# A hybrid encoder block: the side work of the projections' stage queued behind the dense work

## The chip, the core and the metric

The kernel runs on one core of one Trainium2 chip. TensorE (PE) multiplies; VectorE (DVE), ScalarE (ACT) and GpSimd (POOL) do the rest of the arithmetic; SyncE (SP) issues nearly all transfers from one queue. The metric is device time in microseconds (us), the median of three runs.

## The reference

One block: a combined input projection of 2064 tokens feeds two mixers, neighbourhood attention (8 heads) and a bidirectional gated delta rule (4 heads, both directions); their outputs go through an output projection and a SwiGLU feed-forward part. Everything is float32. Cut to what the change touches:

```python
u = rmsnorm(h, g_mix[l])
proj = u @ w_in[l]                       # 1024 -> 3600 columns
na_q, na_k, na_v, dn_q, dn_k, dn_v, dn_z, dn_b, dn_a = jnp.split(proj, pts, axis=-1)
...
qkv = short_conv(jnp.concatenate([q, k, v], axis=-1), conv_w)   # 5 taps, then silu
q = l2norm(q) * (DN_KEY_DIM ** -0.5); k = l2norm(k)
...
diff = gc[..., :, None] - gc[..., None, :]
decay_mat = jnp.where(incl, jnp.exp(jnp.where(incl, diff, 0.0)), 0.0)
m = jnp.where(strict, jnp.einsum('bhnid,bhnjd->bhnij', kb, kc_) * decay_mat, 0.0)
a_mat = m + jnp.eye(CHUNK)
sol = lax.linalg.triangular_solve(a_mat, rhs, left_side=True, lower=True, unit_diagonal=True)
qk = jnp.einsum('bhnid,bhnjd->bhnij', qc, kc_) * decay_mat
...
state, o = lax.scan(step, s0, xs)        # over chunks, forward and backward
```

The kernel works on chunks of 128 tokens, and inverts `a_mat` itself: blocks of 32 by elimination, one matrix to a lane, then two doublings by matrix products.

## The kernel before, in words

There are three stages, one after the other: `phase_a` (projections, and all that can be made of them chunk by chunk), `phase_b` (attention and the scan, in turns) and `phase_c` (output projection and feed-forward). The change is in `phase_a` and its helpers.

**Dense work.** `phase_a` goes over the tokens in two passes, tokens 1024 to 2047 first (half 1), then 0 to 1023 with the meta tokens (half 0). In each pass it goes over 24 units of output columns: 20 "feature" units of 128 columns (12 convolved ones, `dn`, and 8 for attention's keys and queries, `na`) and 4 natural-layout units of 256 or 272 (`v0`, `v1`, `z0`, `z1`). `unit_order` lists them. A feature unit has three column ranges of tokens, a natural one eight or nine tiles of tokens. For each of these, 24 products of split operands (L346, L370) fill one accumulator `acc` of three, and one engine copies it out. Such 24 products are called a dense chunk here; the stage has 186 of them, 92 in half 1 and 94 in half 0, and places on PE are counted in them. `load` and `ahead` ask for the weights of the next two units (`raw`, two buffers); ACT casts them and POOL subtracts (L173 to L175).

**Side work.** Three lists of Python generators hang on the dense work: `post` (after a convolved unit: gate, transposes L582, norms, stores of `dx`), `pre` (`gates`, and four `pre_unit`s: two pairs of heads in two halves) and `first` (row scales, the meta tokens' state). After each dense chunk `tick` runs some steps of each: two of `post`, `n_pre` of `pre` (2 in half 1, 5 in half 0), two of `first`. A step is what stands between two `yield`s. A list works on its first entry alone, when that entry's condition holds.

The convolution of a unit is no side work: `fin` emits it (L438 on ACT, four steps L440 on DVE) behind the unit's last dense chunk, and adds a `post_conv` to `post`: `tanh` and gate (L574, L575), then the transposes.

A `pre_unit` goes over eight pairs of chunks. For each it loads keys and queries (L779) and two row vectors of decays (L784), forms three decay matrices E (L791 on DVE, L793 on ACT, L796 on POOL), stores the scaled queries (L802), multiplies (L806) and scales (L811, L815). The loads have two sets of buffers (`kqs`, `rws`), and those of the row vectors are freed by the store. Then the diagonal blocks go through memory into lanes (`lane`), `invert_lanes` eliminates (62 instructions on DVE, L116 and L117), the blocks come back, and four kinds of small products, each step waiting for the copy of the one before, complete the inverse (L863 to L882, L898, L908 to L910): first for direction 0, then for direction 1.

**What sets the order.** Every engine works strictly in the order of its own queue. The program's text does not set that order alone: a scheduler places each instruction when its own timeline says that the inputs are there, so side instructions may be placed ahead of dense ones that stand earlier in the text.

`fin_v` is called at the end of `v0` and `v1` of half 0: four copies from `vn` to `vx` in memory (L406), 3.8 MB in all.

## Time and profile before

| | |
|---|---|
| runs | 2934.6 to 2936.4 us, median 2935.79 |
| the profiled execution | 2934.77 us, span 2933.1 us |
| PE busy | 2763.0 us (94%) |
| DVE, ACT, POOL busy | 1765.8, 1173.4, 744.6 us (60, 40, 25%) |
| chain that ended last | PE 52%, DVE 3%, DMA 2% |
| mean granted clock of PE | 0.965 of 2.4 GHz |

The page gives shares of the whole span, so an engine at 94% can still stand still in one stage. What a change in one stage is worth is read from that stage: its idle time on PE, and what ended it. Busy times of matmuls overlap one another and say little of how fast they follow. A wait for several things is put down to the one that came last.

### The profile page before, as it was taken

To read this page: it belongs to the slowest core of one execution; us is meant where nothing else is said; L and a number is where in the kernel's file an instruction comes from. 1 tells how busy PE (TensorE), PEld (TensorE's weight loads), DVE (VectorE), ACT (ScalarE), POOL (GpSimd) and SP (SyncE) were. 2 spreads that over 40 slices of the span, in tenths; PEclk is the share of its full clock that TensorE was granted. 3 is DMA by queue.
4 is the path that set the end of the run, shared out by engine and by line. 5 is a ranking of instruction groups with operands and counts; after the bars stand their busy time and mean duration, and the time that the engine had idled before them with its cause. 6 is when DMAs were issued, how large, how long until landed. Compare 5 with 4: busy or idle time off the path is not lost.

```text
span 2933.1 us, 45808 instructions
## 1 busy us (share of the span) xinstructions
PE 2763.0 (94%) x16364; PEld 2415.5 (82%) x16364; DVE 1765.8 (60%) x3908; ACT 1173.4 (40%) x2741; POOL 744.6 (25%) x769
## 2 busy tenths in 40 slices
PE   8989989889898998879999999999999999999998
PEld 8889889888798898877887888887887888888886
DVE  5895766586463555774568655555456665554354
ACT  5653324452324666753234333334334332333342
POOL 2343534142321112231115222310014323220010
PEclk9999999999898999978999999999999999999999
DMA  5675653475669988985545222237443322225452
GB/s 163 189 192 151 175 140 117 146 195 137 187 145 276 295 248 241 287 268 176 189 131 183 87 83 70 78 105 262 140 176 109 100 87 72 87 90 191 142 176 76
DMA packets 398017, 466.32 MB, mean 159 GB/s; under 512 B 91955, under 2 KB 302220, under 8 KB 396222
## 3 DMA queue, kind: packets, MB, share of 16 engines
q1 hardware_dynamic: 396062, 457.11, 51.5%
q0 software_dynamic: 1728, 6.29, 0.6%
q8 instruction: 130, 2.13, 0.3%
q14 instruction: 97, 0.79, 0.1%
HBM read 334.14 MB, written 141.15 MB: 162 GB/s over the span
## 4 chain that ended last, share of the span: by engine, by line
PE 52%; DVE 3%; DMA 2%; issue 1%; ACT 0%; POOL 0%; SPq 0%; DVEq 0%; ACTq 0%; POOLq 0%
PE pg L1522 24%; PE pg L1598 8%; PE pd L1382 6%; PE pd L1598 4%; PE tp L1598 4%; PE pd L1522 4%; DMA rt<-ut 1%; PE y L1062 1%; PE tp L1335 1%; DVE w L1366 0%; PE tp L1408 0%; DMA b<-in_rel_dram 0%; DVE z L1199 0%; DMA k<-kx 0%; DMA z<-zx 0%
## 5 line engine op out<-in xcount | busy, mean ns | idle before, releaser
L346 PE MATMUL acc<-uh,wf 128*128 128x384 f32 (+5 forms) x1920 | 469.3, 330 | 0.0
L1366 DVE TENSOR_TENSOR w<-rw,w 128x512 fp32r<-128x512 f32 x308 | 245.4, 799 | 253.2 <-ACT w L1365 252.1
L1522 PE MATMUL pg<-T,w 128*128 128x512 f32 x1584 | 394.0, 397 | 2.3 <-ACT T L1365 1.3
L1522 PE MATMUL pg<-B,w 128*128 128x512 f32 x1584 | 388.6, 398 | 3.5 <-ACT B L1365 2.9
L1365 ACT CAST w<-rw 128x512 fp32r<-128x512 f32 x308 | 190.2, 620 | 487.1 <-PE tp L1598 253.5
L1522 PEld LDWEIGHTS pg<-B,w 128*128 128x128 f32 x1584 | 299.5, 189 | 77.6 <-ACT B L1365 3.3
L1522 PEld LDWEIGHTS pg<-T,w 128*128 128x128 f32 x1584 | 298.4, 189 | 76.5 <-ACT T L1365 1.7
L346 PEld LDWEIGHTS acc<-uh,wf 128*128 128x128 f32 x1920 | 343.0, 194 | 2.4 <-issue 0.3
L346 PE MATMUL acc<-ul,wf 128*128 128x384 f32 (+5 forms) x960 | 315.8, 329 | 0.0
L1598 PE MATMUL pg<-w,hT 128*128 128x512 f32 x1056 | 260.9, 395 | 1.4 <-ACT hT L1365 1.3
L1470 POOL TENSOR_TENSOR s<-rw 128x512 f32<-128x512 f32 x88 | 116.8, 1328 | 545.6 <-DMA rw<-in_w_gate_dram 278.4
L1598 PEld LDWEIGHTS pg<-w,hT 128*128 128x128 f32 x1056 | 198.0, 188 | 50.3 <-ACT hT L1365 1.7
L1366 DVE TENSOR_TENSOR w<-s,w 128x512 fp32r<-128x512 f32 x176 | 131.0, 747 | 132.3 <-ACT w L1365 131.0
L370 PE MATMUL acc<-wn,uh 128*128 128x256 f32 (+3 forms) x1056 | 207.8, 295 | 0.3 <-ACT uh L288 0.2
L1365 ACT CAST w<-s 128x512 fp32r<-128x512 f32 x176 | 108.7, 621 | 235.2 <-PE pg L1522 141.5
L346 PEld LDWEIGHTS acc<-ul,wf 128*128 128x128 f32 x960 | 186.0, 194 | 1.6 <-DVE ul L289 0.3
L370 PEld LDWEIGHTS acc<-wn,uh 128*128 128x128 f32 (+1 forms) x1056 | 170.9, 195 | 2.7 <-ACT uh L288 0.5
L1382 PE MATMUL pd<-w,yh 128*128 128x512 f32 x512 | 160.9, 396 | 0.0
L370 PE MATMUL acc<-wn,ul 128*128 128x256 f32 (+3 forms) x528 | 156.6, 297 | 2.7 <-DVE rx_i L58 2.7
L440 DVE SCALAR_TENSOR_TENSOR ct<-cr,cw,ct 128x1024 f32<-128x1024 f32 (+1 forms) x96 | 140.4, 1467 | 24.6 <-ACT ct L438 23.8
L175 POOL TENSOR_TENSOR wf<-raw,wf 128x512 fp32r<-128x512 f32 x80 | 109.4, 1381 | 164.1 <-ACT wf L174 160.5
L1536 DVE TENSOR_TENSOR eg<-pg,eg 128x512 f32<-128x512 f32 x110 | 75.9, 690 | 106.0 <-PE pg L1522 106.0
(349 smaller groups left out, 5328.1 us busy)
## 6 DMA issues: line engine op xcount, KB each, us to landing
rw<-in_w_down_dram SPq DMA_DIRECT2D x88, 512.0 KB
rw<-in_w_gate_dram SPq DMA_DIRECT2D x44, 512.0 KB
rw<-in_w_up_dram SPq DMA_DIRECT2D x44, 512.0 KB
hd<-eg SPq DMA_DIRECT2D x88, 256.0 KB
s<-hd SPq DMA_DIRECT2D x88, 256.0 KB
raw<-in_w_feat_dram SPq DMA_DIRECT2D x80, 256.0 KB
w<-dx SPq DMA_DIRECT2D x24, 768.0 KB
xq<-xq SPq DMA_DIRECT2D x32, 512.0 KB
```

What stands on the lines that cost most here:

```text
L175: nc.gpsimd.tensor_tensor(lo, raw, hi, ALU.subtract)
L346: nc.tensor.matmul(ps[:, 0:c1 - c0], hl[:, a, k, :], (U.h, U.l)[l][ci][:, k, c0:c1], start=(i == 0), stop=(i == 23))
L370: nc.tensor.matmul(ps[0:np_, 0:n], (U.h, U.l)[l][ci][:, k, off:off + np_], hl[:, a, k, 0:n], start=(i == 0), stop=(i == 23))
L440: nc.vector.scalar_tensor_tensor(tt, raw[:, j:j + T], cw[:, b, j:j + 1], tt, op0=ALU.mult, op1=ALU.add)
L1062: nc.tensor.matmul(po, t.pT[0:w, c], t.v[0:w, c], start=(c == 0), stop=(c == nch - 1))
L1365: nc.scalar.copy(dst_h, src)
L1366: eng.tensor_tensor(dst_l, src, dst_h, ALU.subtract)
L1382: nc.tensor.matmul(ps, (yh, yl)[a][:, k], wo[k][:, b, cs], start=(i == 0), stop=(i == 23))
L1470: nc.gpsimd.tensor_tensor(s, p, q, op)
L1522: nc.tensor.matmul(ps, w[:, a, k], t[:, b, k], start=(k == 0 and (a, b) == (0, 0)), stop=(k == 3 and a == 1))
L1536: nc.vector.tensor_tensor(dst, ps, x0, ALU.add)
L1598: nc.tensor.matmul(acc[j][hf], hk[f][:, a, j * P:(j + 1) * P], wk[f][hf][:, b], start=(f == 0 and i == 0), stop=(f == NFF - 1 and i == 2))
```

## The change

1. `Behind` notes the last dense-side instruction on PE, DVE and ACT before each tick, and queues every side instruction of that tick behind the one on its engine. SP and POOL get no such order.
2. A tick runs one step of each list; `yield n` asks for n turns before the next step, and a turn is a dense chunk. Entries of `post` are worked on together, no longer one after the other. Pauses after loads are written out (3 turns after the first loads and after the lane load, 4 before the small products).
3. `pre_unit` has four sets of load buffers (`spare` uses the space of `af` and `ab`, which are needed only later), and loads pair n + 4 when pair n is done. In half 0 a pair takes one turn, in half 1 two. In the last unit the elimination is cut into pieces of eight steps, not four.
4. `both` runs directions 0 and 1 in the same steps.
5. In half 0, `v0` stands after the second convolved unit, not after the fourth.
6. `phase_b` keeps the old list under the name `Pieces`.

```diff
+
+    def __init__(self, together=False):
+        self.q = []
+        self.done = 0
+        self.together = together
+
+    def add(self, gen, ready=lambda: True):
+        self.q.append([gen, ready, 0])
+
+    def step(self):
+        for e in list(self.q) if self.together else self.q[0:1]:
+            if not e[1]():
+                continue
+            e[2] -= 1
+            if e[2] > 0:
+                continue
+            try:
+                e[2] = next(e[0]) or 1
+            except StopIteration:
+                self.q.remove(e)
+                self.done += 1
...
+class Behind:
+
+
+    def __init__(self, tc):
+        self.tc = tc
+        self.last = {}
+        self.pos = self.size()
+
+    def size(self):
+        return len(self.tc.nc.cur_bb.bb.instructions)
+
+    def run(self, f):
+        for i in self.tc.nc.cur_bb.bb.instructions[self.pos:]:
+            if i.engine in (mybir.EngineType.PE, mybir.EngineType.DVE, mybir.EngineType.Activation):
+                self.last[i.engine] = i
+        with ExitStack() as es:
+            for i in self.last.values():
+                es.enter_context(self.tc.issue_after(i))
+            f()
+        self.pos = self.size()
+
+
+def invert_lanes(nc, U, Y, T, n, piece=4):
...
         nc.vector.tensor_tensor(Y[:, 0:r, j + 1:n], Y[:, 0:r, j + 1:n], t, ALU.subtract)
-        if j % 4 == 3:
+        if j % piece == piece - 1:
             yield
...
-    return (dn[0:4] + [v0] + dn[4:6] + na[0:1] + dn[6:8] + na[1:2] + dn[8:10] + [v1] + dn[10:11] + na[2:3] + dn[11:12] + na[3:4]
+    return (dn[0:2] + [v0] + dn[2:6] + na[0:1] + dn[6:8] + na[1:2] + dn[8:10] + [v1] + dn[10:11] + na[2:3] + dn[11:12] + na[3:4]
             + [z0] + na[4:8] + [z1])
...
-        post, pre, first = Side(), Side(), Side()
+        post, pre, first = Side(True), Side(), Side()
+        behind = Behind(tc)
 
         def split(hi, lo, src):
...
 
-        def tick(n_pre):
-            post.step(2)
-            pre.step(n_pre)
-            first.step(2)
+        def step():
+            post.step()
+            pre.step()
+            first.step()
+
+        def tick():
+            behind.run(step)
+
+        def drain(*sides):
+            while any(s.q for s in sides):
+                tick()
 
...
-            kind, b, cols, evac, fin, n_pre = units[u]
+            kind, b, cols, evac, fin = units[u]
             c0, c1 = cols[ci]
             evac(ci, dense_feat(u, ci, c0, c1))
-            tick(n_pre)
+            tick()
...
         nc.vector.scalar_tensor_tensor(t[:, a:b], raw[:, a:b], 1.0, t[:, a:b], op0=ALU.add, op1=ALU.mult)
-    yield
-    yield
+    yield 2
     for g in groups:
...
+    spare = [Q.u.tile([P, 16, 64], F32, name=n).rearrange("p (r t) y -> p r (t y)", t=2) for n in ("af", "ab")]
+    kq_of = [kqs[:, 0], kqs[:, 1], spare[0][:, 0:4], spare[1][:, 0:4]]
+    rows_of = [(rws[:, 0], rws[:, 1]), (rws[:, 2], rws[:, 3])] + [(x[:, 4:6], x[:, 6:8]) for x in spare]
+
+    def load(n):
+        a, g = divmod(n, 4)
+        h, cg = 2 * hp + a, c0 + g * 2
+        kq = kq_of[n % 4].rearrange("p (c a) i -> p c a i", c=2)
+        nc.sync.dma_start(kq, S.dx[cg:cg + 2, h, :, 0:2, :].rearrange("c p a i -> p c a i"))
+        for d, row in enumerate(rows_of[n % 4]):
+            src = S.grow[half, d * 4 + h, g * 2:g * 2 + 2, :]
+            nc.sync.dma_start(row, bc(src.rearrange("(o c) i -> o c i", o=1), [P, 2, P]))
+        return kq, rows_of[n % 4]
+
+    def decays(n, kq, rows):
...
+        E = []
+        for e, d in ((0, 0), (1, 1), (2, 1)):
+            ex = Q.g.tile([P, 2, P], F32, name=f"E{e}")
+            for c in range(2):
+                nc.vector.tensor_scalar(ex[:, c], rows[d][:, c], S.gc[:, d * 4 + h, cg + c:cg + c + 1], 0.0,
+                                        op0=ALU.subtract, op1=ALU.max if e == 1 else ALU.min)
+            nc.scalar.activation(ex, ex, AF.Exp, scale=-1.0 if e == 1 else 1.0)
+            if e != 1:
...
+            E.append(ex)
+        for d in range(2):
+            nc.scalar.activation(rows[d], rows[d], AF.Exp)
+            nc.gpsimd.tensor_tensor(rows[d], rows[d], kq[:, :, 0], ALU.mult)
+            nc.sync.dma_start(S.qe[d, cg:cg + 2, h].rearrange("c p i -> p c i"), rows[d])
+        return E
+
+    def grams(n, kq, E):
+        a, g = divmod(n, 4)
+        h, cg = 2 * hp + a, c0 + g * 2
+        pk = Q.pp.tile([P, 2, 2, P], F32, name="pp")
...
+    there = {n: load(n) for n in range(4)}
+    yield 3
+    for n in range(8):
+        E = decays(n, *there[n])
+        yield 1
+        grams(n, there.pop(n)[0], E)
+        if n + 4 < 8:
+            there[n + 4] = load(n + 4)
+        if half == 1:
+            yield 1
...
-    yield
-    yield
+    yield 2
...
-    yield
-    yield from invert_lanes(nc, ul, yl, tl, 32)
+    yield 3
+    yield from invert_lanes(nc, ul, yl, tl, 32, 8 if (hp, half) == (1, 0) else 4)
...
-    yield
-    yield
-    yield
-    for d in range(2):
+    yield 4
+
+    def inner(d):
...
+
+    def outer(d, hf):
+
+        M, A = U[d], (af, ab)[d]
...
+    def both(*gens):
+        for _ in zip(*gens):
             yield
...
+    yield from both(inner(0), inner(1))
+    for hf in range(2):
+        yield from both(outer(0, hf), outer(1, hf))
```

`outer` holds the second half of the old loop body, unchanged. Since a scheduler sets the order, three places of it follow.

DVE, half 0, the second pass's fifth convolved unit (`ct`; E and `qd` are those of the chunk pairs, `krs` and `kss` norms). Before:

```order
L440 SCALAR_TENSOR_TENSOR ct_6484<-cr_6242,cw_154,ct_6484 128x1040 x3
L791 TENSOR_SCALAR E0_6350<-yl_6346,gc_114 128x128 x2
L791 TENSOR_SCALAR E1_6355<-yl_6346,gc_114 128x128 x2
L791 TENSOR_SCALAR E2_6359<-yl_6346,gc_114 128x128 x2
L440 SCALAR_TENSOR_TENSOR ct_6484<-cr_6242,cw_154,ct_6484 128x1040
L811 SCALAR_TENSOR_TENSOR U0_6340<-pp_6396,beta_113,E0_6350 128x128
L811 SCALAR_TENSOR_TENSOR U1_6341<-pp_6396,beta_113,E1_6355 128x128
L811 SCALAR_TENSOR_TENSOR U0_6340<-pp_6396,beta_113,E0_6350 128x128
L811 SCALAR_TENSOR_TENSOR U1_6341<-pp_6396,beta_113,E1_6355 128x128
L815 TENSOR_TENSOR qd_6403<-pp_6396,E0_6350 128x256
L815 TENSOR_TENSOR qd_6406<-pp_6396,E2_6359 128x256
L575 SCALAR_TENSOR_TENSOR ct_6484<-cr_6242,ct_6484 128x528
```

Now:

```order
L494 SCALAR_TENSOR_TENSOR ct_6346<-cr_6215,cw_154,ct_6346 128x1040 x4
L649 TENSOR_SCALAR kss_6222<-kss_6222 128x9
L756 TENSOR_TENSOR beta_113<-beta_113,rk2_119 128x2x8 x2
L69 TENSOR_SCALAR kr_i_6391<-kss_6222 128x9
L757 TENSOR_TENSOR bkd_118<-kd_116,beta_113 128x2x8
L70 TENSOR_SCALAR kr_i_6391<-kr_i_6391 128x9
L73 TENSOR_TENSOR kr_t_6392<-kr_i_6391 128x9
L625 SCALAR_TENSOR_TENSOR ct_6346<-cr_6215,ct_6346 128x528
L74 TENSOR_TENSOR kr_t_6392<-kr_t_6392,kss_6222 128x9
L625 SCALAR_TENSOR_TENSOR ct_6346<-cr_6215,ct_6346 128x512
```

Numbers in the names tell buffers apart. Before, three pairs of E steps stand between the third and the fourth convolution step. Now the four steps stand together, the unit's own norms follow, and the first E comes later in the queue.

DVE, half 1, the last convolved unit (`yl` and `tl` are the elimination). Before:

```order
L440 SCALAR_TENSOR_TENSOR ct_4818<-cr_4763,cw_154,ct_4818 128x1024
L117 TENSOR_TENSOR yl_3627<-yl_3627,tl_3628 128x19x13
L440 SCALAR_TENSOR_TENSOR ct_4818<-cr_4763,cw_154,ct_4818 128x1024
L116 TENSOR_TENSOR tl_3628<-yl_3627,ul_3626 128x240
L440 SCALAR_TENSOR_TENSOR ct_4818<-cr_4763,cw_154,ct_4818 128x1024
L117 TENSOR_TENSOR yl_3627<-yl_3627,tl_3628 128x20x12
L440 SCALAR_TENSOR_TENSOR ct_4818<-cr_4763,cw_154,ct_4818 128x1024
L116 TENSOR_TENSOR tl_3628<-yl_3627,ul_3626 128x231
L117 TENSOR_TENSOR yl_3627<-yl_3627,tl_3628 128x21x11
L575 SCALAR_TENSOR_TENSOR ct_4818<-cr_4763,ct_4818 128x512
L116 TENSOR_TENSOR tl_3628<-yl_3627,ul_3626 128x220
L575 SCALAR_TENSOR_TENSOR ct_4818<-cr_4763,ct_4818 128x512
```

Now:

```order
L494 SCALAR_TENSOR_TENSOR ct_4343<-cr_4232,cw_154,ct_4343 128x1024 x4
L869 SCALAR_TENSOR_TENSOR U0_3833<-pp_4381,beta_113,E0_4323 128x128
L869 SCALAR_TENSOR_TENSOR U1_3834<-pp_4381,beta_113,E1_4328 128x128
L869 SCALAR_TENSOR_TENSOR U0_3833<-pp_4381,beta_113,E0_4323 128x128
L869 SCALAR_TENSOR_TENSOR U1_3834<-pp_4381,beta_113,E1_4328 128x128
L873 TENSOR_TENSOR qd_4388<-pp_4381,E0_4323 128x256
L873 TENSOR_TENSOR qd_4391<-pp_4381,E2_4332 128x256
L625 SCALAR_TENSOR_TENSOR ct_4343<-cr_4232,ct_4343 128x512
L845 TENSOR_SCALAR E1_4425<-yl_3839,gc_114 128x128 x2
L625 SCALAR_TENSOR_TENSOR ct_4343<-cr_4232,ct_4343 128x512
```

Before, elimination steps stand between all convolution steps. Now the four stand together, chunk-pair work follows them, and the elimination starts after.

SP, half 1, loads of a `pre_unit`: `ul` and `yl` are the old buffers, `af` and `ab` the spare ones. Before:

```order
L802 DMA qe<-yl 128x2x128 x2
L816 DMA xq<-qd 128x2x128
L779 DMA ul<-dx 128x2x256
L784 DMA yl<-grow 128x256
L816 DMA xq<-qd 128x2x128
L784 DMA yl<-grow 128x256
```

Now:

```order
L856 DMA qe<-ab 128x2x128 x2
L832 DMA ab<-dx 128x2x256
L874 DMA xq<-qd 128x2x128 x2
L835 DMA ab<-grow 128x256 x2
L856 DMA qe<-yl 128x2x128
L220 DMA raw<-in_w_feat_dram 128x512 x2
L856 DMA qe<-yl 128x2x128
L874 DMA xq<-qd 128x2x128 x2
```

Before, the load into `ul` and `yl` stands right behind the store that reads `yl`, and the next pair waits for it. Now the loads into `ab` are for the pair four further on.

## Rows read from the trace of the kernel before

**Rows 1.** Busy time by stretch: us, PE, PEld, DVE, ACT, POOL, clock, DMA.
```profile
0.00:911.60 911.60, 815.82 (x6668) 785.76 (x6668) 593.09 (x1424) 366.48 (x963) 308.67 (x351) 0.94 0.59 164
911.60:1336.00 424.40, 369.07 (x2816) 356.50 (x2805) 261.75 (x997) 264.45 (x851) 104.75 (x180) 0.90 0.93 270
1336.00:2933.10 1597.10, 1578.14 (x6897) 1273.27 (x6895) 910.95 (x1487) 542.43 (x927) 331.15 (x238) 0.99 0.38 127
```

**Rows 2.** Who PE waited for, projections (0 to 911.6 us): total, times, longest.
```profile
PE tp L582 <- DVE ct L575: 31.1, 11, 7.9
PE pp L806 <- DMA ul<-dx: 25.1, 13, 4.4
PE tp L582 <- DVE nat L591: 7.2, 1, 7.2
PE pp L806 <- DVE U L811: 4.8, 1, 4.8
PE pp L908 <- DVE zs L900: 4.1, 1, 4.1
...
PE pp L898 <- DVE af L891: 2.7, 1, 2.7
PE pp L863 <- DMA af<-lane: 2.5, 3, 1.0
...
PE pp L910 <- DVE zs L900: 1.7, 2, 1.1
...
```

**Rows 3.** Who DVE waited for, projections.
```profile
DVE E L791 <- DMA yl<-grow: 57.7, 25, 16.9
```

**Rows 4.** Groups of instructions of DVE, projections: busy us, mean ns, idle before.
```profile
L440 DVE SCALAR_TENSOR_TENSOR ct<-cr,cw,ct 128x1024 f32<-128x1024 f32 (+1 forms) x96 | 140.4, 1467 | 24.6 <-ACT ct L438 23.8
L791 DVE TENSOR_SCALAR E<-yl,gc 128x128 f32<-128x128 f32 x192 | 60.0, 367 | 57.8 <-DMA yl<-grow 57.7
...
L575 DVE SCALAR_TENSOR_TENSOR ct<-cr,ct 128x512 f32<-128x512 f32 (+1 forms) x48 | 36.7, 782 | 13.4 <-ACT cr L574 13.3
L811 DVE SCALAR_TENSOR_TENSOR U<-pp,beta,E 128x128 f32<-128x128 f32 x128 | 36.2, 339 | 7.1 <-POOL E L796 2.7 <-POOL wf L175 2.4 <-PE pp L806 1.0
L815 DVE TENSOR_TENSOR qd<-pp,E 128x256 f32<-128x256 f32 x64 | 25.5, 411 | 8.0 <-DMA xq<-qd 8.0
```

**Rows 5.** Timeline of DVE and PE, the longest wait: start us, us, instruction.
```profile
556.61 4.76 DVE L440 SCALAR_TENSOR_TENSOR ct<-cr,cw,ct 128x1040 f32<-128x1040 f32 x3 [2.64 <-ACT ct L438]
570.47 0.48 DVE L791 TENSOR_SCALAR E<-yl,gc 128x128 f32<-128x128 f32 x2 [9.10 <-DMA yl<-grow]
...
573.16 1.29 DVE L440 SCALAR_TENSOR_TENSOR ct<-cr,cw,ct 128x1040 f32<-128x1040 f32 x1
...
576.82 1.11 PE L582 MATMUL tp<-ident,ct 128*128 128x128 f32 x4 [7.91 <-DVE ct L575]
```

**Rows 6.** Timeline of DVE and PE, an inversion, a convolution, a transpose.
```profile
372.26 0.19 DVE L116 TENSOR_TENSOR tl<-yl,ul 128x31 f32<-128x31 f32 x1 [10.67 <-DMA ul<-lane]
...
394.53 1.28 DVE L440 SCALAR_TENSOR_TENSOR ct<-cr,cw,ct 128x1024 f32<-128x1024 f32 x1
...
401.86 1.12 PE L582 MATMUL tp<-ident,ct 128*128 128x128 f32 x4 [6.03 <-DVE ct L575]
```

**Rows 7.** Timeline of SP and ACT, vn copies, weight loads and the cast.
```profile
544.23 2.81 SPq L406 DMA_DIRECT2D vx<-vn  x4
...
722.19 1.93 SPq L406 DMA_DIRECT2D vx<-vn  x3
...
728.18 0.91 SPq L173 DMA_DIRECT2D raw<-in_w_nat_dram  x2
...
744.59 1.26 ACT L174 CAST wn<-raw 128x512 fp32r<-128x512 f32 x2 [12.11 <-DMA raw<-in_w_nat_dram]
```

**Rows 8.** Timeline of PE, the end of the stage.
```profile
912.59 1.11 PE L898 MATMUL pp<-U 64*64 64x64 f32 x16
...
921.01 0.39 PE L1119 MATMUL z<-S,w 128*128 128x128 f32 x2
```

166 lines of the change are left out of this document (67 added, 99 removed).

## The prediction, made before the changed kernel was run

> **What bounds the kernel now.** I read the page first, then the busy time by stretch, then who waited for whom, then the rows around the longest waits. By stretch [rows 1] the program has three stages: projections up to 911.6 us, attention and scan up to 1336.0, feed-forward to the end. TensorE (PE) is idle for 911.6 - 815.8 = 95.8 us in the first, which is the only one that the diff touches; in the last it is idle for 19 us of 1597. VectorE (DVE) is busy for 593 of 911.6 us there (65%), ScalarE (ACT) 366, GpSimd (POOL) 309: no other engine is full on the average. So the first stage is bounded by PE's own work plus 95.8 us in which PE stands still, plus what the clock loses: the mean grant there is 0.94, so 2 x 0.06 x 911.6 = 109 us run at the lower level of 1.2 GHz, which costs about 55 us. The profiled execution took 2934.8 us, 1.0 below the median of 2935.8; the sum is made against 2934.8.
>
> Who PE waited for [rows 2] shows that no dense matmul waits for its weights or its buffers beyond a few us at the start. It is side work that stands at the head of PE's queue before its input is there: transposes of the convolved units (L582) waited 31.1 us for DVE and once 7.2 us for a copy, products of the chunks (L806) 25.1 us for the load of their chunk and 4.8 us for a buffer that DVE had not read, and the triangular products (L863 to L910) 2.5 + 2.7 + 4.1 + 1.7 = 11.0 us. The other 16.6 us lie in smaller rows, half of them at the start, and stay.
>
> Why DVE is late at 65% load: it works strictly in its queue's order, and side instructions that wait stand in front of others. DVE waited 57.7 us for row loads [rows 3]. The longest wait of PE (7.91 us, until 576.82) is made so: three of four convolution steps run from 556.61, then E stands in the queue and waits 9.10 us for its row load, and the fourth step runs only at 573.16 [rows 5]. The next one at PE (6.03 us, until 401.86) ends another way: an inversion, itself 10.67 us late because its lanes landed late, takes turns with the convolution, whose first step starts at 394.53 [rows 6].
>
> **The change, term by term.** No arithmetic is removed or added, and the instruction counts stay; what changes is who stands before whom.
>
> Four chunk buffers. A chunk's three loads were issued one step ahead of its use, behind the store that frees the buffer; now four chunks are in flight and a load is issued four chunks (eight in the first pass) before its use. At 911.6 / 186 = 4.9 us for a dense chunk that is some 20 us of lead. Of the 25.1 us [rows 2] I take 22 as gone; ends 0 and 25.1.
>
> Side work behind dense work. The transposes keep their places on PE, counted in dense chunks, within about one chunk; so what goes is not their place but DVE's lateness. The two waits explained above are gone (7.9 + 6.0 = 13.9 us): the convolution's four steps now stand together, and inversion steps and E stand behind them. Of the other 17.2 us I take half, 8.6, since the DVE work between a unit's first convolution step and its last gate step falls only a little. So 22.5 us of 31.1; ends 0 and 31.1. The 7.2 us stay: there ACT stood 12.11 us before a cast of weights whose load, issued at 728.18, came behind four copies of vn to vx (the last three from 722.19) [rows 7]; that order is not touched. The 4.8 us stay too.
>
> Both directions together. Each of the four units of chunk work had two rows of triangular steps one after the other, each step on PE waiting for the copy of the one before; now one row of steps of twice the width. Half the waits, at the same wait each: 11.0 / 2, rounded to 6. Ends 0 and 11.0.
>
> Together 22 + 22.5 + 6 = 50.5 of the 95.8 us. **Clock:** the grant falls with PE's waits (0.94 in the stage where PE is idle for a tenth, 0.99 in the one where it is idle for a hundredth [rows 1]), so I give back the same share: 55 x 50.5 / 95.8 = 29 us. Ends 0, if the waits that stay are those that cost the clock, and 39, by the upper ends of the three terms.
>
> The end of the stage. Before, the last unit's triangular products (L898, then L910) still run from 912.59 on, amid attention, and the scan's first product comes at 921.01 [rows 8]. Now they stand ahead of the last dense matmul. PE's time for them is only moved; the scan can start up to 9 us sooner. I take 4.
>
> New wait. In the second pass each dense chunk now carries a whole chunk of side work. By the means of the groups [rows 4] one such chunk costs DVE 6 x 0.367 + 4 x 0.339 + 2 x 0.411 = 4.4 us, and two convolutions (4 x 1.467 + 2 x 0.782 = 7.4 us each) fall into the same eight chunks: 35 + 15 = 50 us of DVE against 8 x 4.5 = 36 us of PE. DVE falls 14 us behind; three buffers of products cover about half. I add 7; ends 0 and 14. The first pass has two dense chunks for each, and room.
>
> Inversion in larger pieces (8 steps for one unit), the meta tokens' longer pauses and the scan's queue under its new name move nothing that PE waits for now: 0, covered by the lead of the same queues.
>
> Sum: -22 - 22.5 - 6 - 29 - 4 + 7 = -76.5 us; 2934.8 - 76.5 = **2858 us**.
>
> **A rule beside it.** The 9.10 us row load landed late behind the first four copies of vn to vx, issued from 544.23 [rows 7]; the change moves the unit that issues them (v0) earlier, to before the third convolution unit. In my sum that wait ends. The Trainium skill (Trainium Kernel Development and Optimization, Key Constraints) says that DMAs from all queues run on the same 16 engines and interleave; by that rule the copies' cost is moved, not removed. Rows 7 agree for the second set of copies, which held up a weight load.
>
> **Rivals.** (1) The copies' wait moves with them: they fall on the weight loads of the next units, and PE waits as long as now (7.9 us, and about 4 us of clock): 2858 + 12 = 2870. For: rows 7. Against: weights are asked for two units ahead.
>
> (2) DVE is the bound: its work is the same, the transposes stand where they stood, so the 31.1 and 11.0 us stay and only the loads' wait goes. -22, clock 55 x 22 / 95.8 = -13, end -4, new wait +7: 2903. For: 4.4 us of DVE for a dense chunk of 4.5. Against: rows 5 and 6, where DVE was idle or busy with work nobody waited for.
>
> (3) Nearly all goes: 25.1 + 31.1 + 7.2 + 11.0 + 4.8 = 79 us, clock 45, end 9: 2802. Against: the 7.2 us has a cause that stays.
>
> (4) Slower: SP's single queue. Chunk loads now stand in it earlier, each behind the store that frees its buffer, and weight loads stand behind those. A late weight load stops ACT at its cast, the copies of finished dense chunks wait behind it, and PE stops when its three accumulators are full, as once now: 12.11 us at ACT [rows 7] gave 7.2 us at PE [rows 2], with some 4 us of clock 11.2 together. The saving of 76.5 us is eaten by the seventh such stall; with eight the time is 2948. For: all loads share one queue. Against: the weights of all 48 units come now with one such stall.
>
> (5) The edges pin what the scheduler did anyway: no change, 2935. Against: the order, where the rows do move.
>
> **How the numbers follow.** Forecast 0.50, its own range 2825 to 2890 from the ends of its terms; (1) 0.15; (2) 0.15; (3) 0.08; (4) 0.07; (5) 0.05. A difference of 0.2% (5.9 us) is about what a measurement of this kernel can tell from none. Faster: 0.50 + 0.15 + 0.15 + 0.08 = 0.88; the same 0.05; slower 0.07. The range 2815 to 2910 takes in the forecast with its bounds, (1), (2) and the upper part of (3); it leaves out (4), (5) and the rest of (3), some 0.17.
>
> **What would show it.** In the profile after: attention's first product some 75 us sooner, near 835; PE's idle time before it near 50 us instead of 95.8; a mean grant near 0.97; the wait of L806's successor for chunk loads under 5 us and DVE's for row loads well under 57.7; the 7.2 us wait beside the copies still there. The prediction is wrong if the transposes still wait 30 us for DVE (then rival 2), if ACT waits more than now for weights and dense matmuls wait for accumulators (4), or if the mean grant stays at 0.94 though the idle time falls (then the clock's term fails, and the time is near 2887).

## The result, and the profile after

The changed kernel took 2921.78 us in the median of five runs (2913.63 to 2925.80), the kernel before 2935.79: a ratio of 0.9948, 95% interval 0.9929 to 0.9967. Two later comparisons of the same two kernels gave 0.9977 and 0.9959, so the gain is about 0.4%, some 11 us. Forecast were 2858 us with a range from 2815 to 2910: the direction held, the size did not. Some 14 us came where 76.5 were expected, and the time lies above the range, between rival 2 (2903) and rival 5 (no change, 2935).

Busy time by stretch of the profiled execution after (span 2920.1 us), for the three stages; the columns are those of [rows 1]:

```profile
0.00:898.40 898.40, 813.03 (x6733) 789.01 (x6734) 611.28 (x1427) 364.36 (x965) 313.12 (x355) 0.94 0.61 167
898.40:1324.00 425.60, 366.23 (x2747) 352.34 (x2746) 261.78 (x995) 264.39 (x851) 100.36 (x176) 0.92 0.91 269
1324.00:2920.10 1596.10, 1577.23 (x6890) 1273.55 (x6887) 907.42 (x1486) 541.39 (x926) 332.28 (x238) 0.99 0.38 127
```

The first stage is 13.2 us shorter (911.6 to 898.4), the rest is as long as it was. PE stands still for 898.4 - 813.0 = 85.4 us in it, against 95.8, and the mean granted clock, as a share of 2.4 GHz (the grant, below), is 0.94 as before: neither the waits nor the clock did what was forecast.

Who PE waited for in that stage, after:

```profile
PE tp L631 <- DVE ct L625: 36.4, 11, 6.1
PE tp L781 <- DMA nat<-mkT: 7.2, 1, 7.2
PE acc L424 <- DVE vs L468: 6.2, 1, 6.2
PE pp L930 <- DMA af<-lane: 5.0, 2, 3.9
PE pp L947 <- issue: 4.1, 1, 4.1
PE acc L400 <- issue: 3.6, 1, 3.6
PE pp L949 <- issue: 2.4, 1, 2.4
PE pp L948 <- issue: 2.3, 2, 2.1
PE tp L631 <- DVE nat L636: 2.1, 3, 1.0
...
PE pp L968 <- issue: 1.8, 1, 1.8
...
PE tp L631 <- DVE nat L640: 1.5, 1, 1.5
...
```

Against [rows 2], the rows of the chunks' products (L806 there, L864 here) are gone, 25.1 + 4.8 us. The transposes (L582, now L631) wait for DVE's gate (`ct`) 36.4 us where it was 31.1, in eleven waits as before. And there are rows with next to no counterpart: 14.2 us with no releaser (0.5 before), that is, waits marked "issue", for which the profile names nothing that ended them, all beside small triangular products; a dense matmul that waits 6.2 us for an accumulator; the meta tokens' transposes, 7.2 us for a load (0.7 before). All rows together, in groups:

| PE waited in the first stage for | before | after |
|---|---|---|
| the chunks' products | 30.2 | 0 |
| transposes of the convolved units, all rows | 42.3 | 40.0 |
| triangular products, for copies and loads | 12.0 | 5.3 |
| no releaser | 0.5 | 14.2 |
| dense matmuls, for accumulators and inputs | 2.9 | 10.1 |
| the meta tokens | 1.9 | 8.9 |
| the rest | 5.7 | 6.7 |

The second line is the fair comparison of the transposes. The wait beside the copies of vn to vx, 7.2 us, was a row of its own before (`nat` L591); its successor at 716.71, 5.4 us, is one of the eleven of the 36.4. Without it, 31.1 us before stand against 31.0 after.

VectorE no longer waits for row loads, 57.7 us in [rows 3]: no such row is left. First in its list, and in ScalarE's, stand now:

```profile
DVE ct L494 <- ACT ct L492: 38.9, 8, 9.6
```

```profile
ACT wn L221 <- DMA raw<-in_w_nat_dram: 68.4, 23, 11.8
...
ACT wf L221 <- DMA raw<-in_w_feat_dram: 39.4, 18, 7.6
```

The convolution (L494) waits for its first step on ACT (L492), and ACT stands 107.8 us before weight loads (100.7 before). The timeline of the longest transposes' wait shows the two hang together, on ACT, DVE and PE:

```profile
135.40 0.62 ACT L221 CAST wf<-raw 128x512 fp32r<-128x512 f32 x1 [7.59 <-DMA raw<-in_w_feat_dram]
135.92 1.15 ACT L492 ACTIVATE ct<-cr,cw 128x1024 f32<-128x1024 f32 x1
```

```profile
137.11 6.22 DVE L494 SCALAR_TENSOR_TENSOR ct<-cr,cw,ct 128x1024 f32<-128x1024 f32 x4 [6.58 <-ACT ct L492]
143.25 1.26 DVE L845 TENSOR_SCALAR E<-yl,gc 128x128 f32<-128x128 f32 x6
144.42 1.29 DVE L625 SCALAR_TENSOR_TENSOR ct<-cr,ct 128x512 f32<-128x512 f32 x2
```

```profile
145.17 1.11 PE L631 MATMUL tp<-ident,ct 128*128 128x128 f32 x4 [6.09 <-DVE ct L625]
```

The four convolution steps do stand together, as the order said. They come late because a cast of weights stands ahead of their first step on ACT.

The next places have other causes. At 479.92 (5.29 us) elimination steps (L162, L163) and convolution steps (L494) take turns again, as this piece of DVE's timeline shows:

```profile
470.64 1.30 DVE L494 SCALAR_TENSOR_TENSOR ct<-cr,cw,ct 128x1040 f32<-128x1040 f32 x1
471.85 0.40 DVE L162 TENSOR_TENSOR tl<-yl,ul 128x240 f32<-128x240 f32 x1
472.17 2.51 DVE L494 SCALAR_TENSOR_TENSOR ct<-cr,cw,ct 128x1040 f32<-128x1040 f32 x2
474.59 0.40 DVE L163 TENSOR_TENSOR yl<-yl,tl 128x240 f32<-128x240 f32 x1
```

At 716.71 (5.39 us) ACT waited 11.81 us for weights, issued at 699.84 behind the copies of vn to vx: the wait that [rows 7] showed before, and that was forecast to stay. The timeline of ACT and PE:

```profile
714.04 0.62 ACT L221 CAST wn<-raw 128x512 fp32r<-128x512 f32 x1 [11.81 <-DMA raw<-in_w_nat_dram]
```

```profile
716.71 0.66 PE L631 MATMUL tp<-ident,ct 128*128 128x128 f32 x2 [5.39 <-DVE ct L625]
```

### The profile page after: what moved, and what is told of

It reads as the page before. It is cut to its first block, busy times and chain, and to the rows that moved or that the text cites. A ratio compares the mean times of both kernels' runs of the same rounds, so it can differ in the third digit from the quotient of the medians.

```text
span 2920.1 us, 45810 instructions
## 1 busy us (share of the span) xinstructions
PE 2756.5 (94%) x16364; PEld 2414.9 (83%) x16364; DVE 1780.5 (61%) x3908; ACT 1170.1 (40%) x2741; POOL 745.8 (26%) x769
## 3 DMA queue, kind: packets, MB, share of 16 engines
q8 instruction: 130, 2.13, 0.3%
## 4 chain that ended last, share of the span: by engine, by line
PE 68%; DVE 11%; DMA 11%; issue 4%; ACT 2%; POOL 2%; SPq 1%; DVEq 0%; ACTq 0%; POOLq 0%
PE pg L1599 24%; PE pg L1675 8%; PE pd L1459 6%; PE acc L400 4%; PE pd L1675 4%; PE tp L1675 4%; PE acc L424 4%; PE pd L1599 4%; DVE ct L494 2%; PE y L1139 2%; DMA b<-in_rel_dram 2%; DMA qr<-qx 1%; DMA raw<-in_w_nat_dram 1%; DVE tl L162 1%; DVE yl L163 1%
## 5 line engine op out<-in xcount | busy, mean ns | idle before, releaser
L494 DVE SCALAR_TENSOR_TENSOR ct<-cr,cw,ct 128x1024 f32<-128x1024 f32 (+1 forms) x96 | 140.6, 1467 | 40.4 <-ACT ct L492 38.9
L1613 DVE TENSOR_TENSOR eg<-pg,eg 128x512 f32<-128x512 f32 x110 | 75.9, 690 | 107.2 <-PE pg L1599 107.2
```

What stands on the lines that cost most here:

```text
L494: nc.vector.scalar_tensor_tensor(tt, raw[:, j:j + T], cw[:, b, j:j + 1], tt, op0=ALU.mult, op1=ALU.add)
L1613: nc.vector.tensor_tensor(dst, ps, x0, ALU.add)
```

## The experiments

All of them in one table, from the profile of each: the end of the first stage (attention's first product), PE's idle time in it, its mean grant, the transposes' waits for DVE's gate, the waits without a releaser, the scan's first product, and the ratio of the timed runs to the kernel before with its interval. The labels are those of the headings below.

| kernel | stage | idle | clock | transposes | no releaser | scan | ratio |
|---|---|---|---|---|---|---|---|
| before | 911.6 | 95.8 | 0.94 | 31.1 | 0.5 | 921.0 | 1 |
| after | 898.4 | 85.4 | 0.94 | 36.4 | 14.2 | 904.5 | 0.9948 (0.9929, 0.9967) |
| c_after | 898.6 | 78.8 | 0.93 | 35.3 | 14.3 | 904.4 | 0.9977 (0.9961, 0.9993) |
| c_after2 | 903.6 | 87.3 | 0.93 | 35.4 | 17.4 | 909.2 | 0.9959 (0.9944, 0.9974) |
| e1 | 864.5 | 78.1 | 0.96 | 34.4 | 0 | 952.3 | 1.0155 (1.0132, 1.0178) |
| e2 | 909.0 | 90.8 | 0.93 | 33.3 | 9.9 | 914.5 | 0.9983 (0.9968, 0.9998) |
| e3 | 888.9 | 79.7 | 0.95 | 31.9 | 14.4 | 894.0 | 0.9953 (0.9926, 0.9980) |
| e4 | 907.0 | 86.4 | 0.93 | 26.5 | 16.4 | 910.7 | 0.9991 (0.9977, 1.0004) |
| e5 | 906.3 | 88.2 | 0.93 | 40.8 | 10.7 | 907.9 | 1.0017 (1.0006, 1.0028) |
| e6 | 901.0 | 84.2 | 0.94 | 37.5 | 7.1 | 907.4 | 1.0000 (0.9984, 1.0017) |
| e7 | 901.1 | 89.6 | 0.95 | 24.6 | 13.1 | 906.2 | 0.9988 (0.9974, 1.0001) |
| e8 | 874.5 | 64.7 | 0.95 | 24.1 | 5.6 | 878.6 | 0.9860 (0.9844, 0.9876) |
| e9 | 881.1 | 87.3 | 0.95 | 33.4 | 4.5 | 923.5 | 1.0056 (1.0039, 1.0074) |
| e10 | 922.2 | 107.8 | 0.92 | 44.0 | 13.1 | 942.5 | 1.0112 (1.0080, 1.0144) |
| e11 | 914.5 | 107.2 | 0.94 | 38.9 | 15.5 | 934.8 | 1.0069 (1.0047, 1.0092) |
| e12 | 885.2 | 80.0 | 0.96 | 26.7 | 10.9 | 890.6 | 0.9942 (0.9928, 0.9957) |
| e12 again | 888.5 | 76.7 | 0.95 | 29.4 | 12.0 | 894.2 | 0.9960 (0.9943, 0.9977) |
| e13 | 893.2 | 80.1 | 0.95 | 26.5 | 15.1 | 896.6 | 0.9940 (0.9921, 0.9959) |
| e14 | 900.3 | 79.1 | 0.94 | 33.9 | 9.6 | 903.6 | 0.9949 (0.9931, 0.9967) |
| e15 | 940.8 | 95.2 | 0.91 | 36.9 | 27.8 | 944.8 | 1.0099 (1.0070, 1.0127) |

In e1, e9, e10 and e11 a part of the last unit's small products runs behind the end of the stage (PE has 6284, 6284, 6620 and 6620 matmuls in it, the change 6733), so their first two columns count less work. The medians of one kernel differ by some 4 us from chip to chip and its ratios by 0.3% (the three of the change), so a smaller difference between rows of different chips says nothing. c_after, e9, e10 and e11 share a chip; so do c_after2, e12, e13 and e14; e1 to e4; e5 to e8; and e15 and e12 again.

**The controls.**

> The changed kernel itself once more, beside the three others on the same chip, so that they can be compared with it: a ratio to the kernel before of 0.993 to 0.997 again, whatever the theory; a run's spread of some 6 us is expected of each.

> The changed kernel once more, as the control of the three others on the same chip; the two earlier ratios to the kernel before were 0.9948 and 0.9977, so 0.994 to 0.998 is expected whatever the theory.

Both as expected. They show how far profiles of one kernel differ: 78.8 to 87.3 us of idle time for stages of 898 to 904 us. The places of the long waits are the same in all three.

**Are the waits without a releaser the bursts?** (e1, e5, e15) e1 takes the directions apart:

```diff
-    yield from both(inner(0), inner(1))
+    yield from inner(0)
+    yield from inner(1)
     for hf in range(2):
-        yield from both(outer(0, hf), outer(1, hf))
+        yield from outer(0, hf)
+        yield from outer(1, hf)
```

> The changed kernel with the triangular steps of direction 0 ahead of those of direction 1 again, all else as in the change. Theory A (the bursts of twice as many small products run PE out of instructions: in the changed kernel 14.2 us of PE's waits have no releaser, all just behind such a burst, each beside a load of PE's instruction queue): these waits fall under 4 us, the half-clock time around them goes too, and the time is 12 to 18 us under the changed kernel, about 2907. Rival B (the waits without a releaser belong to the place in the program, and the two directions together save half the waits for copies): they stay, the waits for copies come back, and the time is 2922 to 2930.

On the waits theory A held: none is left. On the time both theories missed: attention began at 864.5, 34 us sooner than in the change, and the kernel as a whole was 1.8% or more above it. The busy time by stretch and the timelines of DVE, GpSimd and PE in e1 show where:

```profile
864.50:952.30 87.80, 29.25 (x485) 26.54 (x483) 36.89 (x103) 11.77 (x28) 12.13 (x19) 0.53 0.48 129
```

```profile
887.03 0.19 DVE L162 TENSOR_TENSOR tl<-yl,ul 128x31 f32<-128x31 f32 x1 [14.22 <-DMA ul<-lane]
```

```profile
910.46 1.90 POOL L898 COPY ul<-yl 128x1024 f32<-128x1024 f32 x1 [35.72 <-DVE yl L163]
```

```profile
919.36 0.88 PE L1127 MATMUL y<-ident,sb 128*96 128x128 f32 x3 [54.06 <-ACT sb L1120]
...
952.29 0.79 PE L1198 MATMUL z<-S,w 128*128 128x128 f32 x2
```

With one direction after the other each unit takes more turns, and the last unit's side work did not fit ahead of the last dense matmul. Its elimination starts at 887.03 (820.25 in the change), and attention's softmax stands behind it in VectorE's queue and behind the lane copy in GpSimd's: PE waits 54.06 us for its result. PE was busy for 29 of the next 88 us until the scan's first product, at a grant of 0.53; the scan began 48 us later than in the change. So the two directions together do something that no term of the prediction had: they keep the end of the stage in place, at the price of the bursts.

e5 delays only the second step of direction 1 by one chunk, not in the last unit (an excerpt; `both` is rewritten too, so that one direction may run on when the other is done):

```diff
         yield
+        if d == 1 and (hp, half) != (1, 0):
+            yield
         p = Q.pp.tile([P, 16, 32], F32, name="pp")
```

> The changed kernel, both directions still together, but the second of the small steps (48 products for each direction) one dense chunk later for direction 1; not in the last of the four units, so that the end of the stage stays. Theory A (PE runs out of instructions in the burst of 96 products): the waits without a releaser behind that step (2.4, 4.1 and 3.6 us in the first three units) fall under 1 us each, some of the half clock behind them goes, the end of the stage moves back by at most one dense chunk, and the time is 8 to 20 us under the changed kernel (ratio to the kernel before 0.988 to 0.992). Rival B (the first step's 64 products are enough to empty it): the waits stay or move to the first step, ratio 0.994 to 0.997.

Rival B held: 10.7 of 14.2 us stay, at the same places (4.1 us at 512.8, 3.5 at 736.4), and the transposes waited 4 us longer. The ratio, 1.0017, is above what either theory said. e15 doubles the suspect instead:

```diff
-            nc.tensor.matmul(z[32:64, c], M[0:32, c, 32:64], y0, start=True, stop=True)
-            nc.tensor.matmul(z[96:128, c], M[64:96, c, 96:128], y2, start=True, stop=True)
+            for _ in range(2):
+                nc.tensor.matmul(z[32:64, c], M[0:32, c, 32:64], y0, start=True, stop=True)
+                nc.tensor.matmul(z[96:128, c], M[64:96, c, 96:128], y2, start=True, stop=True)
...
-            nc.tensor.matmul(p[32:64, c], y1, z1, start=True, stop=True)
-            nc.tensor.matmul(p[64:96, c], z3, y3, start=True, stop=True)
+            for _ in range(2):
+                nc.tensor.matmul(p[32:64, c], y1, z1, start=True, stop=True)
+                nc.tensor.matmul(p[64:96, c], z3, y3, start=True, stop=True)
```

> The changed kernel with most of the small products of the first two steps issued twice (the second writes the same result; 128 products more in each of the four units, each run as two matmuls and two weight loads, so some 512 instructions of PE more). Theory A (PE runs out of instructions: its queue is loaded 16 KB at a time, and in the changed kernel two loads in a burst followed 3.3 us after one another while some 18 us lie between them elsewhere): each unit needs two such loads more in the same burst, the waits without a releaser rise from 14 to 17 us to 30 us or more, and the time by 25 to 50 us. Rival B (those waits come from something else in the burst, and the products cost what they measure, some 18 ns a matmul): the waits stay under 20 us, and the time rises by about 19 us of products alone.

Theory A, a little short: 27.8 us without a releaser (30 expected, 20 at most for the rival), and the ratio 1.0099 is 1.4% above the mean of the change's three, some 40 us. Three rows of who PE waited for in the first stage of e15:

```profile
PE pp L950 <- issue: 9.4, 3, 5.1
PE pp L951 <- issue: 8.1, 4, 2.8
...
PE pp L948 <- issue: 6.2, 2, 5.1
```

The trace of the change shows what lands before such a wait ends. The timeline of PE has a product start after 4.06 us; the transfers by queue show, for the first 1.6 us of that wait and then for the rest of it, what moved (queue, packets, MB, share):

```profile
516.43 0.21 PE L947 MATMUL pp<-zs,ab 32*32 32x32 f32 x1 [4.06 <-issue]
```

```profile
q1 hardware_dynamic: 55, 0.36, 53.8%
...
q1 hardware_dynamic: 58, 0.48, 47.7%
q8 instruction: 1, 0.02, 2.3%
```

One packet of the instruction queue q8 lies in the second part (514.0 to 516.4; the packet itself from 514.15 to 515.03) and none in the first. All of q8's packets are 16 KB (the page of the change has 130 with 2.13 MB). In the change, the two controls and e15 there are 24 waits of this kind over 0.9 us; 23 have such a load beside them, and PE goes on 1.2 to 1.8 us after the load has ended. That the loads are the cause is read from this timing, from e1 and from e15; no run changed the loads themselves. In dense work these loads follow one another at some 18 us; in the burst at 301.5 two came 3.3 us apart.

**Does the place, the order or the buffers matter?** (e2, e3, e4) e2 puts `yield 3` for `yield 2` ahead of the transposes in `post_conv`.

> The changed kernel with the transposes of a convolved unit one dense chunk later (a pause of three turns in place of two). Theory A (the transposes stand at a place with no slack: each of the eleven waits for DVE is between 1.0 and 6.1 us, and one chunk of 4.8 us covers most of it): 36.4 us of waits fall to about 5, the grant of the clock follows, and the time is 2870 to 2890. Rival B (DVE is the bound and falls further behind whatever the place): the waits stay at 30 or more, the time stays within 6 us of 2922.

Rival B: 33.3 us of 36.4 stay. But the edit moved the transposes by less than it says: counted in the dense matmuls ahead of them on PE, those at the change's waits stand from 0.3 of a chunk sooner to 1.0 later, and at 479.92 not at all. So what a whole chunk would give is not shown. The waits moved: the 6.09 us wait is 1.4 in e2, but where 3.9 us stood at 293.6 there are 8.7 now. There the row scales (L315) stand between the convolution steps of VectorE, in both kernels; the first of them waited 2.15 us for a row load in e2 and 2.02 us for GpSimd in the change. The timeline of DVE in e2:

```profile
282.85 1.61 DVE L315 TENSOR_TENSOR xe<-xe,gb 128x128 f32<-128x128 f32 x1 [2.15 <-DMA gb<-rs]
284.38 1.27 DVE L494 SCALAR_TENSOR_TENSOR ct<-cr,cw,ct 128x1024 f32<-128x1024 f32 x1
285.58 2.92 DVE L315 TENSOR_TENSOR xt<-xt,gb 128x1024 f32<-128x1024 f32 x1
288.42 2.98 DVE L494 SCALAR_TENSOR_TENSOR ct<-cr,cw,ct 128x1024 f32<-128x1024 f32 x1
```

e3 leaves `Behind` in place and lets it set nothing:

```diff
-            for i in self.last.values():
+            for i in ():
                 es.enter_context(self.tc.issue_after(i))
```

> The changed kernel without the order that queues side work behind dense work on PE, DVE and ACT; turns, buffers and directions as in the change. Theory A (that order only swaps one set of late transposes for another: 31.1 us before, 36.4 now): the time stays within 8 us of 2922, with more waits of DVE for row loads and less of ACT in front of convolutions. Rival B (the order is what brings the gain): the time goes back to 2935 or above.

Theory A on the time: 0.9953, the same as the change within some 8 us. What it said of DVE's row loads came true with 8.0 us only, of the 57.7 before. So the order behind dense work is worth nothing measurable, and the most of the row loads' waits went with the buffers and the pauses.

e4 uses two of the four sets (`n % 2` for `n % 4`, and pair n + 2 is loaded in place of n + 4).

> The changed kernel with two sets of chunk buffers instead of four, each loaded as soon as the pair before in it is done. Theory A (the 29.4 us of waits at the chunks' products went because of the four buffers): 15 to 30 us of waits come back at the chunks' products, most in the second pass where a pair takes one dense chunk, and the time is 2935 to 2955. Rival B (they went because of the pauses in turns and the order alone): no waits at the chunks' products, 2922 within 6.

Between the two: 9.7 us of waits at the chunks' products come back, in the second pass, where 15 to 30 were expected; 0.9991 stands 0.1 to 0.4% above the three ratios of the change. So of the 25.1 us some 15 went with the earlier issue and the pauses, some 10 with the number of buffers.

**What keeps the transposes late?** (e6, e7, e8, e10) e7 moves the weights' cast to GpSimd:

```diff
-            nc.scalar.copy(hi, raw)
+            nc.gpsimd.tensor_copy(hi, raw)
```

> The changed kernel with the casts of the projections' weights on GpSimd in place of ScalarE (GpSimd takes some 150 us more, of 313 busy in 898). Theory A (ScalarE stands 107.8 us at the head of its queue for weights, and the convolution's first step and the tanh behind it make the transposes late): the transposes' 36.4 us of waits for VectorE fall to some 20, and the time is 15 to 30 us under the changed kernel. Rival B (they are late by VectorE's queue itself): they stay above 30, the time stays within 8 us, or rises where GpSimd becomes late with weights.

Half of theory A: the transposes' waits fall to 24.6 us, 11.8 less, and the time does not follow (0.9988). The idle time is 89.6 us all the same. A wait taken away from one row of PE's list turned up in others.

e6 is e5 with the copy of the lanes (`tensor_copy(ul, ...)`) on VectorE.

> The kernel of the split second step, with the copy that turns the eliminated lanes (between the elimination and the loads that bring it back) on VectorE in place of GpSimd. Theory A (GpSimd stands 29 us at the head of its queue before that copy, the weights' subtractions and so the next weight loads wait behind it, ScalarE then 11.8 us for weights and PE 5.4 us for transposes near 716): that wait of PE falls under 2 us, and the time is 5 to 12 us under the split kernel. Rival B (the transposes there are late by VectorE's own work): the wait at that place stays above 4 us and the time is the same within 5 us.

Rival B as far as the number goes (5.36 us at 717.30 stay), but not for its reason: ACT still waits there for the weights. Their load is issued at 700.5, when the subtraction at 699.1 has freed its buffer, and lands 14 us later beside the vn copies. The 29 us that GpSimd stood before the lane copy were not the cause.

e8 stops the elimination after 8 of 31 columns, so its output is not the inverse (an excerpt):

```diff
+        if n < 32 or j < 8:
-        nc.vector.tensor_tensor(t, ...)
-        nc.vector.tensor_tensor(Y[:, 0:r, j + 1:n], ...)
+            nc.vector.tensor_tensor(t, ...)
+            nc.vector.tensor_tensor(Y[:, 0:r, j + 1:n], ...)
```

> The changed kernel with the elimination of the 32 x 32 blocks stopped after 8 of 31 columns (46 of 62 instructions of VectorE left out in each of the four units, some 80 of 611 us; the pauses stay, the output is not the inverse). Theory A (VectorE is not the bound; only the waits that the elimination makes by standing between convolution steps go, 5.3 us near 480, and those near 716 that hang on its end): the time falls by 8 to 20 us. Rival B (VectorE's load is what makes the transposes late): the transposes' waits fall under 12 us, and the time by 35 us or more.

Between the two: the transposes' waits fall to 24.1 us, and the stage by 24 us for 73 us less of VectorE. The ratio of 0.986 is 0.9 to 1.2% under the change's three, 26 to 34 us. Some 15 us of that lie in the second stage (422.8 us from attention's first product to the output projection's, against 437.6). That is no mark of e8: the profiled execution of e13, whose elimination is whole, has 422.2 there, and the other kernel of its chip, e12, 441.7. What makes that stage so long or so short was not found. e10 keeps the work and moves it to GpSimd (`nc.gpsimd` for `nc.vector` where n is 32).

> The changed kernel with the elimination of the 32 x 32 blocks on GpSimd in place of VectorE (108 us off VectorE's 611; GpSimd has 313 busy of 898). Theory A (VectorE's load makes part of the transposes late, as the run with a short elimination showed, 24 us of the stage): the transposes' waits fall as there, by 10 us or more, and the time by 5 to 20 us. Rival B (GpSimd's queue is as touchy: the weights' subtractions stand behind the elimination there, weights come late, ScalarE stands longer before its casts): ScalarE's waits for weights rise above 130 us and the time is 10 us or more above the changed kernel.

Rival B: ACT waits 138 us for weights, the transposes 44.0 us, the time is 1.35% above the control. Taking 95 us off VectorE and putting them into another queue that weights depend on made the same transposes later.

**v0's place.** (e11) `dn[0:4] + [v0] + dn[4:6]` again in the second pass.

> The changed kernel with the second pass's first natural-layout unit (v0) after the fourth convolved unit again, as before. Theory A (its place only moves four copies of 3.8 us in all and the gates; no wait of PE above 2 us hangs on it): the time within 6 us of the changed kernel. Rival B (with the copies at the old place a row or weight load is late again): one wait of 5 us or more near the third convolved unit of the second pass, and the time 8 us or more above.

Both wrong: 0.9% above the control, and not by the copies. The last dense matmul stands at 898.4, as in the control, but attention begins at 914.5 and the scan at 934.8, 30 us later: the last unit's steps come too late, as in e1 (its elimination ends at 872.9, in the control at 849.7). v0 carries the columns of the gates, which the chunk work needs.

**Can the bursts go at no cost?** (e9, e12, e13, e14) e9 takes the directions apart in the first pass alone, with pieces of eight in the second.

> The changed kernel with the directions one after the other in the two units of the first pass, where there is room before the second pass needs them, and together in the second; the elimination there in pieces of eight steps in both units, to win back four dense chunks. Theory A (the bursts of both directions cost waits without a releaser and half clock; with all four units apart the first pass took 9.7 us less, and the loss lay in the last unit's tail alone): the first pass ends 8 to 12 us sooner than at 437.5, the tail stays, and the time is 5 to 15 us under the changed kernel. Rival B (the room is not there: pieces of eight steps and a later start of the second pass's units make VectorE later): the second pass takes that back, the time within 5 us of the changed kernel or above it.

The first pass ended at 428.2, as theory A said. The tail did not stay: scan at 923.5. e12 wins the room where it is lost:

```diff
-        if half == 1:
-            yield 1
...
+    if half == 1:
+        yield from inner(0)
+        yield from inner(1)
+        for hf in range(2):
+            yield from outer(0, hf)
+            yield from outer(1, hf)
+    else:
+        yield from both(inner(0), inner(1))
```

> The changed kernel with the directions one after the other in the two units of the first pass, and a pair of chunks in one turn there instead of two, so that the second pass's units start as early as in the change and the last one's steps still end ahead of the last dense chunk. Theory A (bursts of both directions cost waits without a releaser, and the runs that took them apart lost only by the last unit's tail): no wait without a releaser of over 1 us in the first pass, which ends some 10 us sooner (428 against 438 to 440), the tail as in the change, and the time 6 to 12 us under the control. Rival B (pairs in every chunk make VectorE later in the first pass, and the transposes' waits grow by as much): the first pass ends within 4 us of the control's, the time too.

> The kernel with the directions apart in the first pass and a pair in one turn there, once more on another chip. Its ratio to the kernel before was 0.9942, the changed kernel's 0.9948, 0.9977 and 0.9959. Theory A (it is a little faster than the change): 0.993 to 0.995 again. Rival B (the difference was the chip's): 0.996 or above.

The tail holds (scan at 890.6), the stage is 18 us shorter than the control's beside it, and the time 0.9942 against 0.9959: 5 us, with intervals that overlap. On the other chip 0.9960. So it is no slower than the change, and whether it is faster is not settled. The first pass ends at 433.2 against 438.4, between what the two theories said. Two waits without a releaser stay in it. One, 4.0 us at 268.38, stands behind a burst: the order has the second step of direction 0 and the first of direction 1 in one place. The other, 2.4 us at 176.43, stands at the chunks' products, and the last instruction load had ended 5.1 us before PE went on, so it is not of the kind above; its cause is open.

e13 is e12 with `yield 5` for `yield 3` behind the meta tokens' loads, e14 is e13 without `Behind`, as in e3.

> The kernel of the run beside it (directions apart in the first pass), with a pause of five turns in place of three between the loads of the meta tokens' keys and the transposes and products that use them. Theory A (PE stands 6 to 7 us there for a load that landed late, and the place has room): that wait goes, and the time is 4 to 9 us under that kernel. Rival B (the load lands late because its issue waits in SP's queue behind stores of the chunk pairs, which later turns do not thin out): it stays above 4 us, the time within 3 us.

> The kernel with both edits before it (directions apart in the first pass, meta tokens' pause), and without the order that queues side work behind dense work. Theory A (that order is worth nothing, as the first run without it showed): within 4 us of the kernel with it. Rival B (with single directions it is what keeps the bursts apart and VectorE in time): 8 us or more above it.

e13 could not test its theories, since the wait was no longer there: e12 itself, to which the pause was added, has 0.6 us of it where the control has 6.8. The row of who PE waited for in e12:

```profile
PE tp L781 <- DMA nat<-mkT: 0.6, 1, 0.6
```

The time is the same (0.9940). The profiled execution of e13 is 14 us under that kernel's median, and 6.1 us without a releaser stand near the end of its first stage. In e14 theory A: 0.9949, no difference.

## Why the prediction was wrong, point by point

**Four chunk buffers, -22:** right, and a little low. 25.1 us of waits for loads went, and with them the 4.8 us at L806 that were to stay; DVE's 57.7 us too. e4 shows that some 15 of the 25.1 us need no more than two buffers. By the groups above, what gain there is comes from this term.

**Transposes, -22.5:** the step that failed first, "What goes is not their place but DVE's lateness ... The two waits explained above are gone" in its meaning. The two waits did go, with their causes, and others of the same size stand there: 31.0 us for 31.1 without the wait beside the copies, 40.0 for 42.3 with all rows. So the term measured 0 to 2. The prediction read two of eleven waits, found E and an elimination in the way, and took both causes to be the ones that count. The runs show several causes for one symptom: ACT before a weight load (e7, 12 us), elimination steps (e8, 12 us), row scales (e2). The transposes stand so close behind the convolution that what delays DVE or ACT becomes a wait of PE. The order behind dense work (e3) does not touch that, since side steps of earlier ticks still stand among a later convolution. Rival 2's row (transposes still at 30 us) came true, but its reason only in part: a lighter VectorE helps (e8), and 73 us less of its work gave 24.

**Both directions together, -6:** the saving came, and a larger cost with it. The triangular products' waits fell from 12.0 to 5.3 us, and those that are left are for lane loads. e1, with the directions apart, waits for copies 2.8 us in the first three units and 4.5 in the last one, behind the stage, so the part may well have brought its 6. The waits without a releaser, 14.2 us where it was 0.5, are the cost; saving and cost together are some 7 us the wrong way. The prediction counted waits between steps and not the number of instructions in a step. What the part does buy is turns: without it (e1) the scan begins 48 us later. With v0's place it is the same (e11, 30 us). The sum had 0 for v0 and 4 for the end; in the runs these parts make up for the turns that a schedule of one step in a turn takes.

**Clock, -29:** measured 0. The grant is 0.94 in both; 2 x 0.06 x 898.4 = 108 us at the lower level, 109 before (by the record of the granted clock 109 and 102). The rule that the clock's loss goes by the share of PE's waits failed: the control c_after has 17 us less of idle time than the kernel before (78.8 for 95.8), and 126 us at the lower level for 102. The record of the granted clock has six stretches at 1.2 GHz behind waits at the chunks' products in the kernel before, 27 us in all, which went; and five behind the bursts in the changed one, 31 us, which came. Two of these in the rows of the busy time by stretch, behind the bursts at 301 and 512:

```profile
297.00:311.00 14.00, 11.46 (x225) 10.33 (x224) 2.74 (x4) 2.89 (x5) 3.07 (x3) 0.76 0.40 102
512.40:523.00 10.60, 6.57 (x57) 6.22 (x57) 2.01 (x3) 3.65 (x6) 2.10 (x2) 0.68 0.51 214
```

**End of the stage, -4:** the scan begins 6.1 us behind attention's first product, where it was 9.3: 3.2 us. From attention's first product to the output projection's first it is 437.6 us for 435.8, so none of it arrives in the time.

**New wait, +7:** too small, and at the wrong place. No product of a pair waits for DVE; an accumulator does for 6.2 us at the change of passes, and the meta tokens' load costs 7.2 us for 0.7, 12.7 us together. The load's issue stands in SP's queue behind stores of the pairs. At the change of passes VectorE's second copy of an accumulator (L468, 432.41) stood behind row scales (L315) that waited for GpSimd, which had stood 10.73 us before a load: a dense copy behind side work, which the new order does not forbid.

**The copies and the weights:** 5.4 us at 716.71 for 7.2, as said to stay. The load issued at 699.84 landed 14 us later beside the vn copies. The Trainium skill (Trainium Kernel Development and Optimization, Key Constraints) says that DMAs issued from SP, ACT and POOL all run on the same 16 engines. The 14 us fit that, but the copies and the load were issued from one queue, SP's, so no run here shows it across queues.

PE's idle time fell by 10.4 us and its busy time by 2.8: the 13.2 us of the stage.

**The range.** The forecast's own range, 2825 to 2890 "from the ends of its terms", is not what those ends add up to: all at their best give 2820, all at their worst 2949, and the measured time lies between. The stated range was too narrow for what its terms left open.

## What to carry to other kernels

A wait that a trace shows at the engine that bounds the kernel is a place, not an amount that can be had: where side work stands with no slack behind a queue that has many ways of being late, taking one cause away can move the wait to another place (e2, e7). Before counting on it, look at each of the waits of a row, not at the two longest, and ask which of their causes the change removes. And count the instructions of a step that is made wider: fewer and larger bursts of very small products are not cheaper. Last, parts of one change can be there to pay for each other, as both directions and v0's place are here; the end of a stage has to be priced with each part taken out.

## What had not been expected of the hardware

PE can run out of instructions, as far as the timing shows. A step of both directions is 64 and then 96 small products, and each plain float32 product stands in the trace as two matmuls and two weight loads. Behind such a step PE stood for 1.3 to 6.3 us, until 1.2 to 1.8 us after the next 16 KB load of its instruction queue. Nothing of the kind over 0.5 us is in the kernel before or in e1, where a step has 32 or 48; e15 doubled it to 27.8 us. Such a wait has no releaser in a profile and is named "issue"; not every wait of that name is one (e12, 176.43). The Trainium skill (Runtime: NRT & Kernel Launch, Instruction fetch mechanics) says that such loads of 16 KiB are mostly hidden, since instructions are issued more slowly than they are fetched; the traces here agree for dense work and differ for these bursts.

Bursts with such waits also ran in part at the lower clock, 1.2 GHz: in e15 the grant was 0.91 over the stage, in the stretch of its last burst, with PE busy for 14.86 of 30 us, 0.58, by the busy time by stretch:

```profile
885.00:915.00 30.00, 14.86 (x595) 14.10 (x594) 4.21 (x6) 3.28 (x6) 2.29 (x3) 0.58 0.82 194
```

What stays open: why the second stage is some 15 us shorter in e8 and in e13's profiled execution, and what holds PE's idle time near 80 us when single rows of it go away. The waits that took the place of others stand in each trace's list, but no run shows a common cause.
